# All operands of the matmuls at one remainder modulo 256 bytes, the streams of half products 192 bytes further

## The chip, the cores and the metric

The kernel runs on one NeuronCore of a Trainium2 chip. The metric is the device time of one execution in microseconds; lower is better. PE is the matrix engine, PEld its weight loads, DVE, ACT and POOL the vector, scalar and GpSimd engines, SP the queue that issues most loads.

## The reference

Three transformer-like blocks over 512 tokens of width 1024, all in float32. `first_block` runs twice, `second_block` once:

```python
for l in range(DEPTH):                                        # DEPTH = 2
    x = x + 0.5 * rms_norm(swiglu(rms_norm(x, ..), w_ffn1_in[l], w_ffn1_out[l]), ..)
    mix = token_mixing(rms_norm(x, ..), ..)                   # sliding attention, mLSTM, RWKV-7
    x = x + rms_norm(mix, ..)
    x = x + 0.5 * rms_norm(swiglu(rms_norm(x, ..), w_ffn2_in[l], w_ffn2_out[l]), ..)
    gate = jax.nn.sigmoid(rms_norm(x, ..) @ w_ple_gate[l])
    x = x + rms_norm(gate * (p[l] @ w_ple_proj[l]), ..)
...
x = x + mixed @ w_out                                         # second block: two attentions
x = x + conv_ffn(rms_norm_2(x, norm2_g), w_up, conv_w, conv_b, w_down)
```

The feed-forward width is 2816, so each `swiglu` and the `conv_ffn` has 22 tiles of 128 gate channels, 22 of 128 other channels, and an output product over 22 groups of 128.

## The kernel before, in words

Everything is held on chip between phases: `ffn` (four times), `mix` (twice), `ple` (twice), `block2` with the phase `ffn2` in it.

**Products.** A float32 factor is split into a high and a low part (`split`, L274: ACT writes the high part, DVE the rest), and `mm3` (L284) makes one product of three matmuls, high by high (L287), high by low (L288), low by high (L289). Each matmul loads its own 128 x 128 stationary operand; while one streams its moving operand, PE reads the stationary operand of the next.

**Feed-forward phases.** `norm_fast` writes the normalised tokens, transposed and split, into `xh` and `xl` [128, 8, 512]. Four tiles go the plain way (`proj_t`, the first three of them by token halves, 256 columns at a time). `fast_parts` then makes sums of quarters of the tokens, the tiles `ts`, and `fast_pair` (L451) computes the other tiles two at a time with seven products of halves: 84 matmuls of 256 columns per pair, 48 of which stream `xh` or `xl` and 36 `ts`, in the order 24 of `xh`/`xl`, 36 of `ts`, 24 of `xh`/`xl`. `ahead` (L400) splits the weights of the next pair meanwhile. The four `ffn` phases have 20 such pairs each. The phase `ffn2` has 14 (there the last 12 matmuls of a pair stream a `ts` tile too), and every third pair goes through `tile_t` (L415) instead, 12 tiles of 24 matmuls of 512 columns. `ffn_out` then multiplies by the output weights with tokens on partitions (`proj_n8`): per group of 128 channels 24 matmuls of 512 columns that stream the split weights `wh`, `wl` with the split activations `gs` as stationary operand; the last four groups keep their weights in `wx` tiles.

**Other products.** `mix` and `block2` take `xh`, `xl` from `norm_t`, as moving operand (`proj_t_steps`) or as stationary operand (`proj_n_steps`, `proj_n8`); in `mix` they are woven with the other streams, step by step.

**Order.** Each engine runs its instructions in the order in which the program has them; a matmul waits through a semaphore for the engine that wrote its operands.

**Where the tiles lie.** Pools place their tiles one behind the other in a partition, so a tile's start follows from the sizes of all before it. Remainders of the starts modulo 256 bytes in the program as built:

| tile | before | after |
|---|---|---|
| weights `wh`, `wl` | 96 | 64 |
| `xh`, `xl` from `norm_t` | 32 | 64 |
| `xh`, `xl` from `norm_fast` | 32 | 0 |
| `ts` in the four `ffn` phases / in `ffn2` | 224 / 160 | 0 |
| `gs`, and `wx` of the output products, in the four / in `ffn2` | 224 / 160 | 64 |
| `wx` of `ple` | 224 | 64 |

Steps within these tiles are multiples of 512 bytes, so every matmul on a tile has the remainder of the tile.

Of the kernel before, what the change touches and what calls it, by code (L numbers as in the profile page):

```python
# [85 lines left out]
# per-channel vectors of a layer, [128, n] columns  # L86
PV_OFF, PV_N = _offsets({k: np.zeros((1, n)) for k, n in (
    ("mu", 8), ("w0", 2), ("a0", 2), ("kk", 2), ("ka", 2), ("rk", 2), ("conv", 16))})
# per-token rows of a layer
# [7 lines left out]
def lay_out(inp):  # L97
    """The inputs in the layouts that the kernel loads: reshapes, transposes, slices and joins."""
# [4 lines left out]
    def chans(v):  # [n*128] -> [128, n]  # L103
        return v.reshape(-1, P).T
# [10 lines left out]
    def t_chunks(w):  # [K, n*128] -> [n, 128, 8, 128]  # L115
        return c(w.reshape(KD, P, -1, P).transpose(2, 1, 0, 3))

    def n_chunks(w):  # [K, n] -> [128, K/128, n]
        return c(w.reshape(-1, P, w.shape[1]).transpose(1, 0, 2))

    def halves(w):  # [K, 1024] -> [2, 128, K/128, 512]
        return c(w.reshape(-1, P, 2, 512).transpose(2, 1, 0, 3))
# [30 lines left out]
def staggered(gens, depth, lag):  # L153
    """The generators one after another, up to depth of them at a time, each lag steps behind the one before."""
    todo, live = list(gens), []
    since = lag
    while todo or live:
        if todo and len(live) < depth and (since >= lag or not live):
            live.append(todo.pop(0))
            since = 0  # L160
        for g in list(live):
            if next(g, live) is live:
                live.remove(g)
        since += 1
        yield


def weave(*streams):
    """Advance the generators together, each by its number of steps in turn (a fraction: now and then)."""
# [11 lines left out]
# products between the steps of a stream, and rates of the streams woven together  # L181
LAG, EARLY, OTHERS, DELTA, SLIDING, MLSTM = 24, 1, 2, 1, 1.3, 1
FIRST = 2  # pairs of tiles by classical products; the rest by fast_pair


class Kernel:
    def __init__(self, tc, io, out):
        self.tc, self.nc, self.io, self.out = tc, tc.nc, io, out
        self.order = list("ABCD")  # pairs of banks, those that are free first first
# [4 lines left out]
    # -------------------------------------------------------------- pools and constants  # L194
    def setup(self, es):
# [10 lines left out]
        self.ct = self.const.tile([P, C_N], F32, name="consts")  # L206

        def early_x(t):
# [5 lines left out]
                     lambda: nc.sync.dma_start(self.ct[:, P:], self.io["consts"][:, P:])]  # L214
        self.xh = self.const.tile([P, KD, S], F32R, name="xh")
        self.xl = self.const.tile([P, KD, S], F32R, name="xl")
        self.mhalf = self.const.tile([P, 16], F32, name="mhalf")
        nc.gpsimd.memset(self.mhalf, -0.5)
# [15 lines left out]
    def ring(self, **rings):  # L234
        """Name the pairs of banks that bank() takes in turn."""
        for name, tags in rings.items():
            self.rings[name] = [0, list(tags)]
# [18 lines left out]
    def small(self, n=1, tag=None):  # L256
        bufs = 4 if tag else 8
# [6 lines left out]
    # -------------------------------------------------------------- pieces  # L264
    def rsqrt(self, out, in_, scale, add, tag="rs"):
        """out = (in_ * scale + add) ** -0.5"""
# [6 lines left out]
    def split(self, h, l, src):  # L273
        """h + l = src exactly; each has 12 significant bits."""  # L274
# [9 lines left out]
    def mm3(self, out, a, b, start, stop, **kw):  # L284
        """out += a[0+1]^T b[0+1]"""
# [5 lines left out]
    def norm_begin(self):  # L291
        """Begin on the next of the norms; its tokens may come while the phase before still ends."""
        if self.norms and not self.norming:
            i, fast = self.norms.pop(0)
            self.norming = [self.gain(i), 0]
            self.raw = [self.t4.tile([P, 4, 256], F32, tag="t4", name="raw") for _ in range(2)] if fast else None
# [11 lines left out]
    def norm_token(self):  # L308
        """rms_norm(x) * gain of the next 128 tokens, transposed and split"""
# [23 lines left out]
    def norm_t(self):  # L333
        """The next norm's result, transposed and split: two tiles [128, 8, 512]"""
# [7 lines left out]
    def norm_fast(self):  # L342
        """norm_t, with what fast_parts takes"""
# [29 lines left out]
    def fast_parts(self, pool, ps, keep=False):  # L373
        """What the products of fast_pair take: B[k half][token half] = [[b11, b12], [b21, b22]] gives t1 = b12 - b11,
        t2 = b22 - t1, t3 = b22 - b12 and t4 = b21 - t2"""
# [5 lines left out]
        ts = [[pool.tile([P, 4, 256], F32R, tag=f"T{2 * i + j}", name="ts") for j in range(2)] for i in range(3)]  # L381
# [11 lines left out]
        if keep:  # L393
            t4 = [pool.tile([P, 4, 256], F32R, tag=f"T{6 + j}", name="ts") for j in range(2)]
# [6 lines left out]
    def ahead(self, jobs):  # L401
        """jobs are (what prepares, what takes that and returns what is left to do); each is prepared before the one
        before it does what is left"""
# [11 lines left out]
    def tile_t(self, xs, w, take):  # L415
        p = self.mm_ps()
        for k in range(KD):
            self.mm3(p, (w[0][:, k], w[1][:, k]), (xs[0][:, k], xs[1][:, k]), k == 0, k == KD - 1)
        return lambda: take(p)

    def fast_weights(self, w1, w2):
        """What fast_pair takes of w1 = [a11 a12] and w2 = [a21 a22], chunks [128, 8, 128]: a11, a12, s2, s1, s3, s4
        and a22, with s1 = a21 + a22, s2 = s1 - a11, s3 = a11 - a21, s4 = a12 - s2, each split"""
# [26 lines left out]
    def fast_pair(self, ws, xb, top, low):  # L450
        """[top; low] = [a11 a12; a21 a22]^T B in seven products of halves (Strassen, Winograd's form); the low half's  # L451
        first tokens stay in PSUM."""
# [31 lines left out]
    def proj_t_steps(self, xs, tiles, first=0):  # L484
        """Transposed products: tiles is a list of (chunk [128, 8, 128] in DRAM, what takes the sum).
        The first ones go by token halves, as the later tokens come later."""
# [25 lines left out]
    def proj_n_steps(self, lhs, jobs, ahead=1):  # L512
        """Products with tokens on partitions: lhs(k, t) -> (hi, lo) [128, 128]; the jobs are (w [128, 8, n] in
        DRAM, what takes (token tile, sum), its ring of banks); the pieces of w come some pairs of k ahead."""
# [25 lines left out]
    def proj_n8(self, lhs, w, kn, take, pairs, pool=None, last=4, group=3, ahead=True):  # L540
        """Products with tokens on partitions, up to 1024 columns at once: w [128, kn, n] in DRAM, pairs the
        banks of the tokens, pool(i) two tiles for the pieces of the last group, or None; take(t, sums). With
        ahead the next norm begins before the end."""
# [41 lines left out]
    def post8(self, gain, mul, room):  # L585
        """What takes y [512, 1024]: x += mul * rms_norm(y) * gain; room(t) is a tile [128, 2, 512] for y * gain"""
# [20 lines left out]
    # -------------------------------------------------------------- ffn  # L607
# [5 lines left out]
    def gs(self, pool, n):  # L613
        two = pool.tile([P, 2, S], F32R, tag=f"T{(2, 3, 0, 1, 4, 5)[n % 6]}", name="gs")
        return two[:, 0], two[:, 1]
# [14 lines left out]
    def ffn(self, l, f):  # L630
        nc, io = self.nc, self.io
        base = 8 * l + (0 if f == 1 else 4)
        with self.phase(f"ffn{l}{f}") as pool:
            pairs = self.ffn_banks()
            xs, ps = self.norm_fast()
            gpost = self.gain(base + 1)
            g = [pool.tile([P, 2, S], F32, tag=f"g{j}", name="g") for j in range(KF // 2)]
# [32 lines left out]
    # -------------------------------------------------------------- per-layer embedding  # L670
    def ple(self, l):
        nc, io = self.nc, self.io
        with self.phase(f"ple{l}") as pool:
# [6 lines left out]
            self.split(ph, pl, pt)  # L680
            pr = pool.tile([P, NT, 2, 512], F32, name="pr")
# [27 lines left out]
    # -------------------------------------------------------------- rope tables of the first block  # L709
    def rope_tables(self):  # L710
        self.load_late()
        self.cos = self.const.tile([P, NT, 8], F32, name="cos")
        self.sin = self.const.tile([P, NT, 8], F32, name="sin")
# [3 lines left out]
    def rope_tables_(self):  # L717
        """cos and sin of positions * inv_freq, [128, 4, 8]; the angles are reduced to [-pi, pi] for any
        int32 position: first by multiples of 2 pi 2^11, then of 2 pi, each constant in short parts whose
        products with the counts are exact."""  # L720
# [36 lines left out]
    # -------------------------------------------------------------- token mixing  # L757
    def mix(self, l):
# [3 lines left out]
        with self.phase(f"mix{l}") as pool:  # L762
            tl = lambda name, shape, dt=F32: pool.tile(list(shape), dt, tag=name, name=name)
            pv = tl("pv", [P, PV_N])
            nc.sync.dma_start(pv, io[f"pv{l}"])
            rows = tl("rows", [P, RW_N])
            nc.gpsimd.dma_start(rows, io[f"rw{l}"][0].partition_broadcast(P))
# [10 lines left out]
            omu = tl("omu", [P, 8])  # L778
            V.tensor_scalar(omu, pv[:, PV_OFF["mu"][0]:PV_OFF["mu"][0] + 8], -1.0, 1.0, ALU.mult, ALU.add)
            hb = tl("hb", [P, 4])  # L780
            V.tensor_scalar(hb, pv[:, PV_OFF["w0"][0]:PV_OFF["w0"][0] + 4], 0.5, None, ALU.mult)
            oka = tl("oka", [P, 2])
# [6 lines left out]
            # ---- rwkv: products, token shift  # L789
# [37 lines left out]
            def prepare():  # L827
# [7 lines left out]
                for i in range(2):  # L835
# [21 lines left out]
                    # kk, normalised by head  # L857
# [34 lines left out]
            # ---- rwkv: blocks of 128 tokens, chunks of 64  # L892
# [4 lines left out]
            def group(t):  # L897
# [9 lines left out]
                # heads of one parity share the rows of the array, and have banks of their own  # L907
# [126 lines left out]
                # group norm, bonus, gate  # L1034
# [24 lines left out]
            # ---- the other products  # L1059
# [35 lines left out]
            def others():  # L1095
# [5 lines left out]
                while len(ab) < 2:  # its tiles are prepare's before  # L1101
# [9 lines left out]
            # ---- the three together  # L1111
# [6 lines left out]
            # ---- out  # L1118
# [18 lines left out]
    def sliding(self, pool, qk, va, sinks, out):  # L1137
# [3 lines left out]
        for t in range(NT):  # L1141
            # rope
# [11 lines left out]
            # split, scaled by 1/8 for q, and transposed  # L1154
# [88 lines left out]
    def mlstm(self, pool, X, conv, vo, iff, row, out):  # L1243
# [3 lines left out]
        # gates, tokens on partitions  # L1247
# [7 lines left out]
        # log sigmoid(f) = -log(1 + e), e = exp(-f); log(1 + e) = e * log(w) / (w - 1), w = fl(1 + e)  # L1255
# [8 lines left out]
        # heads on partitions: G = cumsum(log f), a = i - G, M = cummax(a)  # L1264
# [396 lines left out]
```

## Time and profile before

| | us |
|---|---|
| median of three runs | 2948.43 |
| lowest, highest | 2946.67, 2959.89 |
| span of the profiled execution, first to last instruction | 2960.7 |
| PE busy in it | 2898.4 |
| DVE, ACT, POOL busy | 1953.1, 1425.6, 140.3 |

The profile is of one execution; no time other than its span is recorded for it. The page's slices show PE at nine tenths or more from the second on and DMA engines busy between none and four tenths. A busy PE is not PE at its peak: matmuls are pipelined, so the busy times of two that follow each other overlap. Their starts don't.

### The profile page before, as it was taken

How to read it: one execution, taken by the hardware profiler on the slowest of the kernel's cores; microseconds unless marked ns; L12 is line 12 of the kernel's file. 1: busy time of each engine (PE TensorE's matmuls, PEld its weight loads, DVE VectorE, ACT ScalarE, POOL GpSimd, SP SyncE). 2: the span in 40 equal slices, each digit the busy share in tenths (PEclk: the TensorE clock that was granted, in tenths of full speed). 3: DMA queues.
4: the chain of work that ended last, by engine and by line, in shares of the span. 5: the costliest groups of instructions: out<-in, count | busy, mean ns of one | idle time of the engine just before them, and what ended most of it. 6: DMA issues, size and time to landing. Idle time of an engine off the chain costs nothing. (4 is left out here: it accounts for less than half of the span.)

```text
span 2960.7 us, 47335 instructions
## 1 busy us (share of the span) xinstructions
PE 2898.4 (98%) x19000; PEld 2538.6 (86%) x19000; DVE 1953.1 (66%) x3464; ACT 1425.6 (48%) x2784; POOL 140.3 (5%) x169
## 2 busy tenths in 40 slices
PE   7999999999999999999999999999999999999999
PEld 7998887877999878999887877799987877789987
DVE  7884555756888357886345655688635766688853
ACT  5663343343666245555334233456534456566641
POOL 0000000101000000000000000100000220000000
PEclk9999999999999999999999988999999999999999
DMA  4333322002233332333412000233343210313332
GB/s 152 108 122 103 97 81 65 8 8 65 93 115 115 100 103 90 109 107 116 130 56 79 15 8 29 75 107 111 114 128 90 93 43 1 93 62 104 100 101 91
DMA packets 74156, 250.91 MB, mean 85 GB/s; under 512 B 8112, under 2 KB 10416, under 8 KB 73680
## 3 DMA queue, kind: packets, MB, share of 16 engines
q1 hardware_dynamic: 70992, 236.99, 25.2%
q0 software_dynamic: 2944, 10.90, 1.1%
q8 instruction: 149, 2.44, 0.3%
q14 instruction: 71, 0.58, 0.1%
HBM read 245.76 MB, written 2.10 MB: 84 GB/s over the span
## 5 line engine op out<-in xcount | busy, mean ns | idle before, releaser
L276 DVE TENSOR_TENSOR wl<-raw,wh 128x1024 fp32r<-128x1024 f32 (+2 forms) x218 | 259.2, 1193 | 410.1 <-ACT wh L275 408.5
L275 ACT CAST wh<-raw 128x1024 fp32r<-128x1024 f32 (+2 forms) x218 | 223.4, 1026 | 469.9 <-PE psone L289 316.9
L287 PE MATMUL psfast<-xh,wh 128*128 128x256 f32 x1448 | 401.9, 278 | 0.0
L289 PE MATMUL psfast<-xh,wl 128*128 128x256 f32 x1448 | 400.7, 277 | 0.0
L288 PE MATMUL psfast<-xl,wh 128*128 128x256 f32 x1448 | 400.6, 277 | 0.0
L287 PE MATMUL psfast<-ts,wh 128*128 128x256 f32 x1184 | 333.1, 282 | 0.0
L289 PE MATMUL psfast<-ts,wl 128*128 128x256 f32 x1184 | 333.0, 281 | 0.0
L288 PE MATMUL psfast<-ts,wh 128*128 128x256 f32 x1184 | 332.5, 281 | 0.0
L288 PE MATMUL psone<-wl,gs 128*128 128x512 f32 x720 | 284.2, 395 | 0.0
L289 PE MATMUL psone<-wh,gs 128*128 128x512 f32 x720 | 284.1, 395 | 0.0
L287 PE MATMUL psone<-wh,gs 128*128 128x512 f32 x720 | 282.3, 395 | 0.0
L287 PEld LDWEIGHTS psfast<-xh,wh 128*128 128x128 f32 x1448 | 272.0, 188 | 1.3
L288 PEld LDWEIGHTS psfast<-xl,wh 128*128 128x128 f32 x1448 | 272.1, 188 | 0.5
L289 PEld LDWEIGHTS psfast<-xh,wl 128*128 128x128 f32 x1448 | 272.0, 188 | 0.0
L435 ACT CAST wh<-raw 128x512 fp32r<-128x512 f32 x282 | 174.7, 621 | 157.8 <-PE psfast L288 154.2
L287 PEld LDWEIGHTS psfast<-ts,wh 128*128 128x128 f32 x1184 | 222.7, 188 | 0.7 <-ACT top L465 0.7
L289 PEld LDWEIGHTS psfast<-ts,wl 128*128 128x128 f32 x1184 | 222.9, 188 | 0.0
L288 PEld LDWEIGHTS psfast<-ts,wh 128*128 128x128 f32 x1184 | 222.8, 188 | 0.0
L437 DVE TENSOR_TENSOR wl<-raw,wh 128x1024 fp32r<-128x1024 f32 (+1 forms) x188 | 179.1, 953 | 64.9 <-ACT wh L435 64.5
L287 PE MATMUL psmm<-xh,wh 128*128 128x256 f32 (+1 forms) x616 | 206.8, 338 | 0.1
L288 PE MATMUL psmm<-xl,wh 128*128 128x256 f32 (+1 forms) x616 | 205.8, 335 | 0.0
L289 PE MATMUL psmm<-xh,wl 128*128 128x256 f32 (+1 forms) x616 | 204.3, 333 | 0.0
(545 smaller groups left out, 6494.1 us busy)
## 6 DMA issues: line engine op xcount, KB each, us to landing
raw<-f1i SPq DMA_DIRECT2D x88, 512.0 KB, 3.5
raw<-f2i SPq DMA_DIRECT2D x88, 512.0 KB, 3.5
raw<-f1o SPq DMA_DIRECT2D x44, 512.0 KB, 3.7
raw<-f2o SPq DMA_DIRECT2D x44, 512.0 KB, 3.9
raw<-w2u SPq DMA_DIRECT2D x44, 512.0 KB, 3.5
raw<-w2d SPq DMA_DIRECT2D x22, 512.0 KB, 3.9
gain<-gains POOLq DMA_DIRECT2D x19, 512.0 KB, 4.0
raw<-wr SPq DMA_DIRECT2D x16, 512.0 KB, 3.6
```

Of the source, the lines that this page charges most:

```text
L275: self.rounded = self.nc.scalar.copy(h, src)
L276: self.nc.vector.tensor_sub(l, src, h.bitcast(F32))
L287: mm(out, a[0], b[0], start=start, stop=False, **kw)
L288: mm(out, a[0], b[1], start=False, stop=False, **kw)
L289: mm(out, a[1], b[0], start=False, stop=stop, **kw)
L435: nc.scalar.copy(h[:, i], src[:, i])
L437: sub(l, src, h.bitcast(F32))
```

## The change

It computes the same products. Starts of tiles move, by changed tile sizes and by tiles that only fill:

- `consts`, `pv`, `rows`, `hg` and `cv` get longer rows than they use, three small vectors of `mix` become one tile `vecs`, `cos` and `sin` move into `setup`, and tiles called `pad` are added, so that the tiles behind them begin at the remainder 64.
- `xh` and `xl` get 48 more floats (192 bytes), and there are two `places` in them: from 0 for the plain norms, from 48 for the norms of the feed-forward phases. `norm_begin` picks one.
- The tiles of `ts` have 1088 floats instead of 1024 and begin with their float 48; `gs` takes the same tiles from their start.
- `tile_t` makes its product by two halves of 256 columns.
- `small` keeps four buffers instead of eight for untagged tiles of more than one column.
- Comments are gone, which shifts line numbers.

```diff
         self.x = self.const.tile([P, NT, D], F32, name="x")
-        self.ct = self.const.tile([P, C_N], F32, name="consts")
+        self.ct = self.const.tile([P, 2416], F32, name="consts")
...
-        self.xh = self.const.tile([P, KD, S], F32R, name="xh")
-        self.xl = self.const.tile([P, KD, S], F32R, name="xl")
+        xh = self.const.tile([P, KD * S + 48], F32R, name="xh")
         self.mhalf = self.const.tile([P, 16], F32, name="mhalf")
+        xl = self.const.tile([P, KD * S + 48], F32R, name="xl")
+        self.cos = self.const.tile([P, NT, 8], F32, name="cos")
+        self.sin = self.const.tile([P, NT, 8], F32, name="sin")
+        self.const.tile([P, 16], F32, name="pad")
+        self.places = [[z[:, o:o + KD * S].rearrange("p (k n) -> p k n", k=KD) for z in (xh, xl)] for o in (0, 48)]
...
     def small(self, n=1, tag=None):
-        bufs = 4 if tag else 8
+        bufs = 4 if tag or n > 1 else 8
...
             self.norming = [self.gain(i), 0]
+            self.xh, self.xl = self.places[fast]
...
-        ts = [[pool.tile([P, 4, 256], F32R, tag=f"T{2 * i + j}", name="ts") for j in range(2)] for i in range(3)]
+        room = lambda i: pool.tile([P, 1088], F32R, tag=f"T{i}", name="ts")[:, 48:1072].rearrange(
+            "p (k n) -> p k n", k=4)
+        ts = [[room(2 * i + j) for j in range(2)] for i in range(3)]
...
         p = self.mm_ps()
-        for k in range(KD):
-            self.mm3(p, (w[0][:, k], w[1][:, k]), (xs[0][:, k], xs[1][:, k]), k == 0, k == KD - 1)
+        for cs in slice(0, 256), slice(256, 512):
+            for k in range(KD):
+                self.mm3(p[:, cs], (w[0][:, k], w[1][:, k]), (xs[0][:, k, cs], xs[1][:, k, cs]), k == 0, k == KD - 1)
...
-        two = pool.tile([P, 2, S], F32R, tag=f"T{(2, 3, 0, 1, 4, 5)[n % 6]}", name="gs")
-        return two[:, 0], two[:, 1]
+        two = pool.tile([P, 1088], F32R, tag=f"T{(2, 3, 0, 1, 4, 5)[n % 6]}", name="gs")
+        return two[:, 0:S], two[:, S:2 * S]
...
-            cv = pool.tile([P, 4, 44], F32, name="cv")
-            nc.sync.dma_start(cv, io["cv2"].rearrange("p (j m) -> p j m", j=4))
+            cv = pool.tile([P, 4, 56], F32, name="cv")
+            nc.sync.dma_start(cv[:, :, 0:44], io["cv2"].rearrange("p (j m) -> p j m", j=4))
```

The order on the engines is the same but for two places in the phase `ffn2`. On PE, where the first of its `tile_t` tiles begins (`psmm` is its sum in PSUM), before:

```order
L288 MATMUL psfast<-ts,wh 128x256
L289 MATMUL psfast<-ts,wl 128x256
L287 MATMUL psmm<-xh,wh 128x512
L288 MATMUL psmm<-xl,wh 128x512
L289 MATMUL psmm<-xh,wl 128x512
```

and now:

```order
L293 MATMUL psfast<-ts,wh 128x256
L294 MATMUL psfast<-ts,wl 128x256
L292 MATMUL psmm<-xh,wh 128x256
L293 MATMUL psmm<-xl,wh 128x256
L294 MATMUL psmm<-xh,wl 128x256
```

Where 24 matmuls of 512 columns stood per tile, 48 of 256 stand now, 24 for each half of the tokens. On DVE, at the same tiles (`z` are sums of the next pair's weights, `g` the result of the tile), before:

```order
L444 TENSOR_TENSOR z<-raw 128x512
L1587 SCALAR_TENSOR_TENSOR g<-psmm,cv,g 128x511
L437 TENSOR_TENSOR wl<-s,wh 128x1024
L1588 SCALAR_TENSOR_TENSOR g<-psmm,cv,g 128x511
L445 TENSOR_TENSOR z<-raw,s 128x512
```

and now:

```order
L453 TENSOR_TENSOR z<-raw 128x512
L454 TENSOR_TENSOR z<-raw,s 128x512
L1595 SCALAR_TENSOR_TENSOR g<-psmm,cv,g 128x511
L446 TENSOR_TENSOR wl<-s,wh 128x1024
L1596 SCALAR_TENSOR_TENSOR g<-psmm,cv,g 128x511
```

The second subtraction into `z` moved ahead of the work on the tile, by three instructions, six times in the phase.

## Rows read from the trace of the kernel before

**Rows 1.** The page: span, and busy time (share of the span) by engine.

```profile
span 2960.7 us, 47335 instructions
...
PE 2898.4 (98%) x19000; PEld 2538.6 (86%) x19000; DVE 1953.1 (66%) x3464; ACT 1425.6 (48%) x2784; POOL 140.3 (5%) x169
```

**Rows 2.** PE's waits, longest total first: releaser, total us, times, longest.

```profile
PE pstr L321 <- DVE xn L316: 22.1, 15, 10.8
...
```

**Rows 3.** Work per stretch: length, busy us and count per engine, granted clock, DMA share, GB/s.

```profile
240.33:340.76 100.43, 100.43 (x435) 81.34 (x434) 38.65 (x43) 31.26 (x40) 0.00 (x0) 1.00 0.40 121
1475.68:1491.78 16.10, 16.10 (x73) 13.33 (x71) 8.71 (x14) 6.06 (x14) 1.65 (x3) 1.00 0.16 56
1126.78:1143.34 16.56, 16.56 (x72) 13.35 (x71) 11.13 (x17) 9.67 (x18) 1.11 (x2) 1.00 0.30 96
62.26:71.99 9.73, 9.73 (x86) 9.73 (x85) 8.26 (x13) 5.86 (x13) 0.00 (x0) 1.00 0.31 102
```

**Rows 4.** The costliest group of PE over the span: form, count, busy us, mean ns.

```profile
L287 PE MATMUL psfast<-xh,wh 128*128 128x256 f32 x1448 | 401.9, 278 | 0.0
...
```

**Rows 5.** Order of time on PE: start, duration, instruction; ends of the stretches of 512 columns.

```profile
240.33 0.39 PE L287 MATMUL psone<-wh,gs 128*128 128x512 f32 x1
...
340.76 0.40 PE L287 MATMUL psone<-wx,gs 128*128 128x512 f32 x1
...
1110.06 0.39 PE L289 MATMUL psone<-wh,xl 128*128 128x512 f32 x1
...
1126.55 0.39 PE L289 MATMUL psone<-wh,xl 128*128 128x512 f32 x1
1126.78 0.39 PE L287 MATMUL psone<-wx,xh 128*128 128x512 f32 x1
...
1143.34 0.40 PE L289 MATMUL psone<-wx,xl 128*128 128x512 f32 x1
...
1475.68 0.39 PE L287 MATMUL psone<-wx,gs 128*128 128x512 f32 x1
...
1491.78 0.39 PE L289 MATMUL psone<-wx,gs 128*128 128x512 f32 x1
```

**Rows 6.** The same view, first `ffn`: ends of a stretch of `xh`, and of 17 pairs.

```profile
62.28 0.28 PE L287 MATMUL psfast<-xh,wh 128*128 128x256 f32 x1
...
67.73 0.28 PE L287 MATMUL psfast<-ts,wh 128*128 128x256 f32 x1
...
227.64 0.28 PE L287 MATMUL psfast<-xh,wh 128*128 128x256 f32 x1
```

**Rows 7.** The same view, start of the first `ffn`'s first pair.

```profile
45.40 0.28 PE L287 MATMUL psfast<-xh,wh 128*128 128x256 f32 x1
...
48.23 0.29 PE L287 MATMUL psfast<-ts,wh 128*128 128x256 f32 x1
...
52.55 0.28 PE L287 MATMUL psfast<-xh,wh 128*128 128x256 f32 x1
```

**Rows 8.** The same view, `ffn2`: two `tile_t` tiles, an early pair, a late pair.

```profile
2646.68 0.39 PE L287 MATMUL psmm<-xh,wh 128*128 128x512 f32 x1
...
2657.87 0.28 PE L287 MATMUL psfast<-xh,wh 128*128 128x256 f32 x1
...
2667.62 0.28 PE L287 MATMUL psfast<-xh,wh 128*128 128x256 f32 x1
...
2782.38 0.28 PE L287 MATMUL psfast<-xh,wh 128*128 128x256 f32 x1
...
2792.28 0.28 PE L287 MATMUL psfast<-xh,wh 128*128 128x256 f32 x1
```

**Rows 9.** The same view, `ffn2`: the first products behind a stall.

```profile
2737.03 0.39 PE L287 MATMUL psfast<-xh,wh 128*128 128x256 f32 x1
2737.26 0.28 PE L288 MATMUL psfast<-xl,wh 128*128 128x256 f32 x1
2737.37 0.28 PE L289 MATMUL psfast<-xh,wl 128*128 128x256 f32 x1
```

More of the change, by code (lines that the diff above doesn't have):

```diff
@@ L213, in setup @@
         self.late = [lambda: early_x(2), lambda: early_x(3),
-                     lambda: nc.sync.dma_start(self.ct[:, P:], self.io["consts"][:, P:])]
-        self.xh = self.const.tile([P, KD, S], F32R, name="xh")
-        self.xl = self.const.tile([P, KD, S], F32R, name="xl")
+                     lambda: nc.sync.dma_start(self.ct[:, P:C_N], self.io["consts"][:, P:])]
+        xh = self.const.tile([P, KD * S + 48], F32R, name="xh")
         self.mhalf = self.const.tile([P, 16], F32, name="mhalf")
+        xl = self.const.tile([P, KD * S + 48], F32R, name="xl")
[3 more added lines that the diff above has]
+        self.places = [[z[:, o:o + KD * S].rearrange("p (k n) -> p k n", k=KD) for z in (xh, xl)] for o in (0, 48)]
         nc.gpsimd.memset(self.mhalf, -0.5)
@@ L393, in fast_parts @@
         if keep:
-            t4 = [pool.tile([P, 4, 256], F32R, tag=f"T{6 + j}", name="ts") for j in range(2)]
+            t4 = [room(6 + j) for j in range(2)]
         def late():
@@ L636, in ffn @@
             gpost = self.gain(base + 1)
+            pool.tile([P, 32], F32, name="pad")
             g = [pool.tile([P, 2, S], F32, tag=f"g{j}", name="g") for j in range(KF // 2)]
@@ L680, in ple @@
             self.split(ph, pl, pt)
+            pool.tile([P, 32], F32, name="pad")
             pr = pool.tile([P, NT, 2, 512], F32, name="pr")
@@ L711, in rope_tables @@
         self.load_late()
-        self.cos = self.const.tile([P, NT, 8], F32, name="cos")
-        self.sin = self.const.tile([P, NT, 8], F32, name="sin")
         with self.phase("rope"):
@@ L763, in mix @@
             tl = lambda name, shape, dt=F32: pool.tile(list(shape), dt, tag=name, name=name)
[L764 to L767, printed above, removed]
+            pv = tl("pv", [P, 40])
+            nc.sync.dma_start(pv[:, 0:PV_N], io[f"pv{l}"])
+            rows = tl("rows", [P, 800])
+            nc.gpsimd.dma_start(rows[:, 0:RW_N], io[f"rw{l}"][0].partition_broadcast(P))
             lora = tl("lora", [P, 512])
@@ L777, in row @@
                 return rows[:, o:o + n]
-            omu = tl("omu", [P, 8])
+            vecs = tl("vecs", [P, 24])
+            omu, hb, oka = vecs[:, 0:8], vecs[:, 8:12], vecs[:, 16:18]
             V.tensor_scalar(omu, pv[:, PV_OFF["mu"][0]:PV_OFF["mu"][0] + 8], -1.0, 1.0, ALU.mult, ALU.add)
-            hb = tl("hb", [P, 4])
             V.tensor_scalar(hb, pv[:, PV_OFF["w0"][0]:PV_OFF["w0"][0] + 4], 0.5, None, ALU.mult)
-            oka = tl("oka", [P, 2])
             V.tensor_scalar(oka, pv[:, PV_OFF["ka"][0]:PV_OFF["ka"][0] + 2], -1.0, 1.0, ALU.mult, ALU.add)
@@ L1345, in block2 @@
             cc = lambda n: c2[:, C2_OFF[n][0]:C2_OFF[n][0] + C2_OFF[n][1]]
-            hg = tl("hg", [P, 256])
-            nc.gpsimd.dma_start(hg, io["hg2"][0].partition_broadcast(P))
+            hg = tl("hg", [P, 288])
+            nc.gpsimd.dma_start(hg[:, 0:256], io["hg2"][0].partition_broadcast(P))
             b0, b1, b2, b3 = self.order
```

## The prediction

> **What bounds the kernel now.** I read the busy table first: PE is busy 2898.4 us of a span of 2960.7, DVE 1953.1 [rows 1]. PE's waits by releaser come next: the largest, the transposes of the norms waiting for DVE, is 22.1 us in all, and the other 22 entries of that view are smaller [rows 2]. So PE's own pace sets the end nearly everywhere. The work per stretch shows how much cover the other engines leave: in one pair of tiles of the fast products (9.73 us) DVE is busy 8.26 and ACT 5.86; in the first eighteen groups of an output product (100.43 us) DVE is busy 38.65 and the DMA share is 0.40 [rows 3]. The granted clock is 1.00 in both, so nothing here is a clock matter.
>
> The busy time of a matmul in the grouped view (278 ns for `psfast<-xh` [rows 4]) is not its price, since matmuls overlap. The price is the step from one start to the next, which I take from the first and the last row of a stretch and the number of matmuls between them, known from the code. What separates stretches of one shape is where the operands lie. Call D the moving operand's start minus the next stationary operand's start, modulo 256 bytes (both remainders are in the table of the kernel before).
>
> - 512 columns, D = 128: 340.76 - 240.33 over 432 steps is 232.5 ns. D = 192: 1143.34 - 1126.78 over 71 is 233.2. D = 64: 1126.55 - 1110.06 over 72 is 229.0. D = 0: 1491.78 - 1475.68 over 71 is 226.8 [rows 5].
> - 256 columns, D = 192: 67.73 - 62.28 over 48 is 113.5. The ts products (D = 128) behind them bring a whole pair of 84 to (227.64 - 62.28) / 17 pairs = 9.727 us [rows 6], so 36 of them take 9.727 - 5.45 = 4.28 us, 118.8 each.
>
> The two stretches of 71 are the same loop and the same weight tiles `wx`, with 8.71 and 11.13 us of DVE inside [rows 3]; the addresses differ, and 6.4 ns of a step with them. Worst D for 512 columns (192) is best for 256. The change puts 512-column products at D = 0 and products of halves at D = 192.
>
> **A second pace at D = 192.** The first 24 products of the first layer run at (48.23 - 45.40) / 24 = 117.9 ns, also with D = 192 [rows 7]. In the last feed-forward phase a whole pair takes 2667.62 - 2657.87 = 9.75 us early on and 2792.28 - 2782.38 = 9.90 later, 117.9 a step, although neither program nor addresses changed [rows 8]. Between the two lies a start after a stall, where the first step is 0.23 us and the next is 0.11 [rows 9]. So products of halves have two settled paces at the same addresses, 113.5 and 117.9, and the slow one survives from there to the end of that phase. In the four ffn phases it is the ts products at D = 128 that never let a pace stand: each time behind them the stream comes back to 113.5. The change removes exactly these. What a phase falls into at its start it will then keep for its 20 pairs.
>
> **The change part by part.** All of this is PE time with no wait in it, so it shortens the path one for one.
>
> (a) Fast products of the four ffn phases, 80 pairs at 9.727 us now. At the fast pace 84 x 113.5 = 9.534: -15.5 us. At the slow pace 9.904: +14.1. One phase of 20 pairs: -3.9 or +3.5, a swing of 7.4.
>
> (b) The last phase has 14 such pairs, about half at 9.75 and half at 9.90, 137.5 us. Fast: 14 x 9.534 = 133.5, -4.0. Slow: 138.7, +1.1.
>
> (c) `tile_t` cuts its 12 tiles into halves: 288 matmuls at (2657.87 - 2646.68) / 48 = 233.1 ns [rows 8] become 576. Fast: 65.4 against 67.1 us, -1.8; slow 67.9, +0.8. The 288 more weight loads need no term, since in the stretch of pairs PEld is loaded for every 256 columns already and the 113.5 holds with it.
>
> (d) Output products: 432 matmuls per feed-forward phase. Four phases: 100.43 to 432 x 226.8 = 97.98, -2.45 each, -9.8. The fifth has D = 192 now, 233.2: 432 x 6.4 = -2.8. Together -12.6. The last 96 of each phase are at D = 0 already.
>
> (e) Products that take xh from the plain norm: 236 with `wx` at D = 192 now, 236 x 6.4 ns = -1.5; 432 transposed ones in the mix phases from 233.2 to between 226.8 and 231, as they are cut short by other work, -1.7; some 1200 at D = 64, 2.2 ns each, of which I count half for the same reason, -1.3.
>
> (f) One loss: 288 products of halves in the mix phases go from D = 192 to D = 0, which has no long stretch here. The bounds are 113.5 and the worst stretch of 256 columns, (52.55 - 48.23) / 36 = 120.0 [rows 7]: 0 to +1.9, taken +1.0.
>
> (g) Costs at nothing: the norms' writes to the other place of `xh` follow transposes that PE runs behind the last readers anyway; DVE's moved `z` subtraction falls into a pair in which DVE is idle 1.47 us (9.73 - 8.26 [rows 3]), 1.27 at 9.534; the smaller ring of `small` holds the four tiles that one prepare uses; the `cv` load in 176-byte pieces is needed only behind the first tile of products, 24 steps after they begin. If such a cover failed, it would be one wait each, of the size of those counted in [rows 2]. A bare wait of PE on PE behind each pair of tiles in the last phase: six times, between 0 and the 0.11 us by which a first step after a stall is longer, under 0.7 us.
>
> 512 columns and (f): -12.6 - 1.5 - 1.7 - 1.3 + 1.0 = **-16.1**. Halves, all fast: -15.5 - 4.0 - 1.8 = -21.3. The first ffn started slow in the trace with the same addresses and the same order that it keeps, while the pairs behind the start of the last phase are at the fast pace [rows 8]; so I take one phase of five slow: -21.3 + 7.4 = **-13.9**. Sum -30.0 us.
>
> **Against the pages.** The stretches above have a step that depends on where the two operands of PE lie [rows 5]. The Trainium skill's page "SBUF — State Buffer", section "Who interferes with whom", says that PE has two independent read ports and never waits on anyone, and its page "TensorE: Matmul & The Clock Gate", section "Step-by-step: what each phase is for", that loading the next weights takes no read bandwidth from the running matmul. By that rule the change would give nothing, which is the second rival below; the trace does not agree, by 6.4 ns per step between the two `wx` stretches.
>
> **The rivals.** *The slow pace wins.* With three to five of the five phases in the slow pace the halves cost -21.3 + 22.2 = +0.9 to +15.7, and the whole gain is 15.2 to 0.4 us: 2933 to 2948. For it: nothing but a stall resets the pace once the ts products lie at D = 192, and half of the last phase shows it. Against it: the last phase was fast from its start to the stall, for half of its pairs.
>
> *The address is not the cause.* ts, gs and wx are different tiles, and their paces could follow the tile (when it was written, say) rather than its remainder. Then nothing moves but (c): 2947 to 2949. Against it: `wx`, written and used by the same lines in both stretches, runs at 226.8 and at 233.2.
>
> *Slower.* A stream at one D may settle at neither pace but at the worst one of the trace, 120.0 ns [rows 7]: 8472 products of halves (7896 in pairs, 576 tiles' halves) at 120.0 are 1016.6 us against 778.2 + 137.5 + 67.1 = 982.8 now, +33.8 - 16.1 = +17.7: 2966. It decides from (982.8 + 16.1) / 8472 = 117.9 ns on, which is the slow pace itself: any pace above it loses. It is seen only behind D = 128, in one stretch.
>
> **How the numbers follow.** The median of the runs shown is 2948.4, 12.3 below the span of the profiled execution; I take the same difference off both: span 2960.7 to 2930.7, median **2918.4**. Chances: the forecast, with no to two phases slow (2911 to 2926), 0.78; slow pace in three or more 0.13; address no cause 0.05; slower 0.04. The range from 2905 (all fast, all of (e), and a little for the 113.5, whose 48 steps hold the recovery behind ts) to 2938 leaves out some 0.15. Faster by over 0.5% (14.7 us, about what can be told from no change) means below 2933.7: the forecast and a part of three phases slow, 0.82; same 0.14; slower 0.04.
>
> **What would show it.** Right: 432 output products in 98.0 us; the last `wx` stretches unchanged at 226.8; pairs of 84 in either 9.53 or 9.90 us and nothing between, constant through a phase; DVE, ACT and DMA busy times as before. Wrong: output products still over 230 ns (D is no cause), a pace for halves over 118, or pairs that switch between the two paces without a stall.

## The result, and the profile after

| | before | after |
|---|---|---|
| median (times of the runs), us | 2954.16 (2946.67, 2948.43, 2959.89, 2962.16) | 2911.48 (2910.41, 2910.74, 2912.22, 2919.21) |
| span of the profiled execution | 2960.7 | 2917.4 |
| ratio of the times, 95% interval | | 0.9873, 0.9843 to 0.9903 |

Faster by 1.3%. The profiled execution of after is the slowest of its four, and that of before, by its span, is one like its slower two; both have their reason in the rows below. A phase is called slow below when its pairs of 84 run at 9.89 us, fast when they run at 9.52.

The page of after, to be set beside [rows 1]: PE's busy time falls by 45 us, that of DVE and ACT stays, and 288 matmuls have come in.

```profile
span 2917.4 us, 47905 instructions
...
PE 2853.4 (98%) x19288; PEld 2525.3 (87%) x19288; DVE 1952.8 (67%) x3464; ACT 1425.8 (49%) x2784; POOL 141.6 (5%) x169
```

The work per stretch of after (columns as in [rows 3]: length, then busy us and count of PE, PEld, DVE, ACT, POOL, then the granted clock, DMA share, GB/s). First the 432 products of the first output product, the `wx` stretch of the first `ple`, 17 pairs of the first `ffn` and 17 pairs of the third:

```profile
235.38:333.59 98.21, 98.21 (x434) 80.90 (x433) 38.86 (x43) 31.48 (x40) 0.00 (x0) 1.00 0.41 123
...
1113.40:1129.73 16.33, 16.33 (x73) 13.47 (x72) 11.03 (x17) 9.84 (x18) 1.11 (x2) 1.00 0.33 98
...
44.77:206.62 161.85, 161.85 (x1430) 161.84 (x1428) 139.31 (x220) 99.34 (x204) 0.00 (x0) 1.00 0.34 109
1167.23:1335.42 168.19, 168.19 (x1430) 168.19 (x1429) 140.07 (x220) 99.48 (x204) 0.00 (x0) 1.00 0.33 105
```

The first line was 100.43 us in [rows 3], with the same DVE and ACT work inside: 227.3 ns a step instead of 232.5. The second is the stretch that was at D = 192: 72 steps of 226.8 ns now. The last two lines are the same 17 pairs of the same code at the same addresses: 161.85 / 17 = 9.52 us a pair in the first phase (also in the second and fourth), 168.19 / 17 = 9.89 in the third. DVE, ACT and the clock are the same in both. The second pace is there, and one of the four phases has fallen into it.

**The clock.** The two `mix` phases run one program. From the end of the output product before to the first pair of the phase behind it, in before and in after:

```profile
357.13:769.79 412.66, 400.03 (x2638) 331.28 (x2636) 255.95 (x610) 167.92 (x373) 35.28 (x40) 0.98 0.15 46
1492.01:1923.89 431.88, 419.37 (x2638) 346.89 (x2637) 252.40 (x587) 167.42 (x371) 35.03 (x40) 0.93 0.14 44
```

```profile
349.92:762.85 412.93, 400.65 (x2637) 333.69 (x2636) 256.10 (x610) 167.80 (x373) 35.24 (x40) 0.98 0.15 46
1479.68:1893.20 413.52, 400.87 (x2637) 333.83 (x2636) 252.53 (x587) 167.50 (x371) 35.31 (x40) 0.98 0.15 46
```

The second one of before is 19.2 us longer than its twin, at a mean clock of 0.93. The reason is one stretch in which PE is granted 0.50, its 1.2 GHz level; after has it too, shorter. PE was busy without a gap at the full clock ahead of it in both (10.90 of 10.90 us, 10.85 of 10.85). Before, then after:

```profile
1743.00:1753.90 10.90, 10.90 (x84) 9.09 (x85) 4.60 (x16) 6.02 (x21) 1.27 (x1) 1.00 0.01 2
...
1753.90:1805.10 51.20, 51.20 (x239) 39.99 (x238) 17.30 (x63) 12.61 (x40) 1.13 (x1) 0.50 0.00 1
```

```profile
1750.00:1760.85 10.85, 10.85 (x86) 9.11 (x86) 5.43 (x27) 2.06 (x10) 0.00 (x0) 1.00 0.01 2
1760.85:1774.50 13.65, 13.65 (x57) 11.25 (x57) 6.12 (x19) 4.91 (x17) 1.14 (x1) 0.50 0.01 2
```

So of the 43.3 us between the two spans an estimated 18 are clock and not the change: the second `mix` differs by 18.4 us between the two, the first by 0.3. In two later runs below, shift32 and d16, only 3.4 us at 0.50 stand there, and their second `mix` takes 408.5 and 408.1 us. The executions whose times are too low to hold that long stretch compare as 2946.67 and 2948.43 with 2910.41 to 2912.22: 36.4 us between the means of these. That is the worth of the change where no phase is slow. With slow phases in some executions it is less: against the later runs of before the medians of after differ by 32.8 us (2945.78, 2912.97) and 33.1 (2945.30, 2912.23).

### The profile page after: what moved, and what is told of

It reads as the page before. It is cut to its first block, busy times and chain, and to the rows that moved or that the text cites. A ratio compares the mean times of both kernels' runs of the same rounds, so it can differ in the third digit from the quotient of the medians.

```text
span 2917.4 us, 47905 instructions
## 1 busy us (share of the span) xinstructions
PE 2853.4 (98%) x19288; PEld 2525.3 (87%) x19288; DVE 1952.8 (67%) x3464; ACT 1425.8 (49%) x2784; POOL 141.6 (5%) x169
## 3 DMA queue, kind: packets, MB, share of 16 engines
q0 software_dynamic: 2944, 10.90, 1.1%
## 5 line engine op out<-in xcount | busy, mean ns | idle before, releaser
L292 PE MATMUL psfast<-ts,wh 128*128 128x256 f32 x1184 | 328.7, 278 | 0.5
L293 PE MATMUL psfast<-ts,wh 128*128 128x256 f32 x1184 | 328.0, 277 | 0.0
L294 PE MATMUL psone<-wh,gs 128*128 128x512 f32 x720 | 280.2, 389 | 0.0
L292 PE MATMUL psone<-wh,gs 128*128 128x512 f32 x720 | 278.4, 389 | 0.0
L292 PE MATMUL psmm<-xh,wh 128*128 128x256 f32 (+1 forms) x712 | 222.1, 314 | 0.6 <-ACT xh L280 0.4
L293 PE MATMUL psmm<-xl,wh 128*128 128x256 f32 (+1 forms) x712 | 220.9, 311 | 0.0
L294 PE MATMUL psmm<-xh,wl 128*128 128x256 f32 (+1 forms) x712 | 219.6, 309 | 0.0
```

Source lines behind the costliest of these rows:

```text
L292: mm(out, a[0], b[0], start=start, stop=False, **kw)
L293: mm(out, a[0], b[1], start=False, stop=False, **kw)
L294: mm(out, a[1], b[0], start=False, stop=stop, **kw)
```

## The experiments

The theory of the prediction: D, the moving operand's start minus the next stationary operand's, modulo 256 bytes, sets the step; 256 columns at D = 192 have two paces; products of another D between them keep bringing the fast one back. Rivals: the tile counts and not its address; the remainder itself counts and not the difference; the slow phase has another cause.

### map: steps by D alone

One moving tile `M`, one set of stationary tiles `W`, stretches behind a stall each (the first product of each has `K`, which ACT writes from the sum of the stretch before):

```python
for i in range(count):
    sr, mr = srs[i % len(srs)] // 4, mrs[i % len(mrs)] // 4
    w = K[:, sr:sr + 128] if s == 0 and i == 0 else W[:, sr + 128 * (i % 8):sr + 128 * (i % 8) + 128]
    b = mr + 512 * (i % 6)
    mm(p[:, 0:n], w, M[:, b:b + n], start=i == 0, stop=i == count - 1)
```

> This kernel computes none of the reference: it streams one moving tile against one set of stationary tiles, in stretches of 48 to 72 matmuls of one shape with one difference D (moving start minus next stationary start, modulo 256 bytes), each stretch behind a short stall, D in steps of 16 bytes; then stretches of D = 192 with other D ahead and no stall, the same D at other remainders, and two remainders in turn. If D sets the step: 512 columns 226.8 ns at D = 0, 229 at 64, 232.5 at 128, 233.2 at 192, the same when both starts move by 64 or 96 bytes or the moving one by 256; 256 columns at D = 192 either 113.5 or 117.9, one of them for a whole stretch, and at 128 near 119 to 120; a stretch with stationary starts in turn at D = 0 and 192 alternates 226.8 and 233.2. If the remainder itself counts and not the difference, the moved stretches have other steps. If the tile counts and not its address, all stretches of one shape have one step.

The order of time on PE has one row for a stretch: start, duration, count. The last product of a row lasts 0.39 us (512 columns) or 0.28 (256), the rest is steps. 512 columns at D = 64, 192, then 0 and 128 with both starts moved by 96 bytes:

```profile
62.35 10.93 PE L68 MATMUL a512d<-M,W 128*128 128x512 f32 x47
...
157.52 11.12 PE L68 MATMUL a512d<-M,W 128*128 128x512 f32 x47
...
922.15 10.84 PE L68 MATMUL r_512d<-M,W 128*128 128x512 f32 x47
...
940.30 11.07 PE L68 MATMUL r_512d<-M,W 128*128 128x512 f32 x47
```

(11.12 - 0.39) / 46 is 233.3 ns, (10.84 - 0.39) / 46 is 227.2 with the first steps in it. 256 columns at D = 0, 112, 128 and 192:

```profile
205.24 7.24 PE L68 MATMUL a256d<-M,W 128*128 128x256 f32 x59
...
260.03 6.88 PE L68 MATMUL a256d<-M,W 128*128 128x256 f32 x59
...
267.61 7.17 PE L68 MATMUL a256d<-M,W 128*128 128x256 f32 x59
...
299.13 7.11 PE L68 MATMUL a256d<-M,W 128*128 128x256 f32 x59
```

The settled steps (from the ninth on) of all D, ns, in this kernel (D = 0 of 512 columns from the moved stretches):

| D | 0 | 16 | 32 | 48 | 64 | 80 | 96 | 112 | 128 | 144 | 160 | 176 | 192 | 208 | 224 | 240 |
|---|---|---|---|---|---|---|---|---|---|---|---|---|---|---|---|---|
| 512 columns | 226.7 | 231.7 | 233.3 | 233.4 | 228.9 | 231.1 | 233.3 | 231.1 | 232.2 | 233.3 | 234.3 | 233.3 | 233.3 | 234.7 | 233.3 | 233.3 |
| 256 columns | 120.0 | 113.3 | 116.7 | 118.3 | 117.8 | 119.9 | 120.0 | 113.3 | 118.7 | 118.7 | 118.7 | 119.2 | 113.3, 117.8 | 119.3 | 118.3 | 117.2 |

D is the cause: one tile pair, addresses alone changed, and the steps of the kernel come back, 226.7, 228.9, 232.2 and 233.3. With both starts moved by 64 or 96 bytes, or the moving one by 256, they are the same to 1.3 ns. D = 0, the best for 512 columns, is the worst of this table for 256. D = 192 gave 113.3 in 35 stretches and 117.8 in 7, each one pace to its end. One product at D = 0 or 128 between two stretches at D = 192, and 36 at D = 0, 64, 128 or 240, left the pace at 113.3. One at D = 64 was enough to turn it, without any stall, both times that it was tried (48 at D = 192, one at 64, 72 at 192: 113.7, then 117.7 ns):

```profile
800.55 5.51 PE L68 MATMUL ma_256d<-M,W 128*128 128x256 f32 x47
805.90 0.28 PE L68 MATMUL mb_256d<-M,W 128*128 128x256 f32 x1
806.02 8.64 PE L68 MATMUL mc_256d<-M,W 128*128 128x256 f32 x72
```

One expectation fell. With stationary starts in turn the steps were 226, 226, 236, 232 and again, not 226.8 and 233.2 in turn, though their mean, 230.0, is as expected. With moving starts in turn at D = 0 and 192 the steps were 225 to 229, on average 226.7. So D gives the step of a stream in which D is constant; what mixed streams do, it doesn't say, and no run here settles that. Nor does any run show why the difference matters inside PE.

### ts128, gs128, shift32: one part undone, one thing moved

```diff
ts128
-        room = lambda i: pool.tile([P, 1088], F32R, tag=f"T{i}", name="ts")[:, 48:1072].rearrange(
+        room = lambda i: pool.tile([P, 1088], F32R, tag=f"T{i}", name="ts")[:, 32:1056].rearrange(
gs128
-        return two[:, 0:S], two[:, S:2 * S]
+        o = 32 if n < 18 else 0
+        return two[:, o:o + S], two[:, o + S:o + 2 * S]
shift32
-        self.ct = self.const.tile([P, 2416], F32, name="consts")
+        self.ct = self.const.tile([P, 2408], F32, name="consts")
```

> The changed kernel with the ts tiles 64 bytes earlier, so that their products stand at D = 128 as in the kernel before; all else as changed. If D sets the step, a pair of 84 takes 9.73 us again in every phase, with 24 products of xh at 113.5 ns behind each group of ts products and no phase at 9.89; 94 pairs by 9.727 - 9.534 are 18.1 us more than the 2910.4 us of the changed kernel with all phases fast, 2928 us. If the slow phase has another cause than the missing return, one of the phases may still stand at 9.89. If the address is no cause: 2910 to 2919, as the changed kernel.

> The changed kernel with the gs tiles of the first 18 groups of every output product 128 bytes further, so that their 432 matmuls per phase stand at D = 128. If D sets the step: 232.5 ns against 226.8, 5 x 432 x 5.7 = 12.3 us more, 100.4 us per stretch of 432 instead of 98.0 and 2923 us with all halves fast (each slow phase 7 more). If the address is no cause: no difference, 2910 to 2919 us.

> The changed kernel with every tile behind the constants 32 bytes earlier: all remainders differ, no difference D does. If only D counts: 2910 to 2919 us as the changed kernel, the steps the same to 0.3 ns. If the remainder itself counts (128 x 512 of the moving operand from 32 instead of 64), steps of the 512-column products differ from 227 by up to some ns: 2160 x 2 ns would be 4 us and more. The number of phases at 9.89 us a pair may differ between executions in either case.

Measured beside 14 runs of before with a median of 2946.29: ts128 2929.53 to 2933.64, median 2931.76; gs128 2924.16 to 2940.02, median 2927.60; shift32 2905.13 to 2941.85, median 2913.13. The stretches that answer, in this order: 17 pairs of ts128 (third phase), the first 432 output products of gs128, those of shift32 and its first 17 pairs.

```profile
1177.20:1342.56 165.36, 165.36 (x1429) 165.35 (x1428) 139.61 (x220) 99.38 (x204) 0.00 (x0) 1.00 0.30 107
```

```profile
234.02:334.49 100.47, 100.47 (x435) 81.17 (x434) 38.81 (x43) 31.49 (x40) 0.00 (x0) 1.00 0.39 123
```

```profile
234.96:333.18 98.22, 98.22 (x434) 80.88 (x433) 38.85 (x43) 31.52 (x40) 0.00 (x0) 1.00 0.41 123
44.35:206.19 161.84, 161.84 (x1429) 161.84 (x1428) 139.35 (x220) 99.45 (x204) 0.00 (x0) 1.00 0.33 109
```

ts128: 165.36 / 17 = 9.73 us, the pace of [rows 6], and that in all four phases: neither 9.52 nor 9.89 occurs in them, but for 9.87 in the last pair of each, which has a stall in it. gs128: 100.47 us, back to [rows 3]. shift32: other remainders everywhere and the steps of after to 0.01 us per stretch; its three executions above 2920 us have mean clocks of 0.979 to 0.985, the other seven 0.992 and more. The rivals of the tile and of the remainder itself fall; two parts of the change are undone one by one, each at its price.

### entry, d16, d0, after_again: which D for the halves

Since D = 16 had given 113.3 three times out of three and settled within two steps, I took it for a D with one pace, and for a better place for the halves than 192. `entry` is the streaming kernel with 20 entries behind stalls of different length; d16 and d0 move the places of the changed kernel:

```diff
d16
-        ... for o in (0, 48)]
+        ... for o in (0, 4)]
-        room = lambda i: pool.tile([P, 1088], F32R, tag=f"T{i}", name="ts")[:, 48:1072].rearrange(
+        room = lambda i: pool.tile([P, 1088], F32R, tag=f"T{i}", name="ts")[:, 4:1028].rearrange(
d0
-        ... for o in (0, 48)]
+        ... for o in (0, 0)]
-        room = lambda i: pool.tile([P, 1088], F32R, tag=f"T{i}", name="ts")[:, 48:1072].rearrange(
+        room = lambda i: pool.tile([P, 1088], F32R, tag=f"T{i}", name="ts")[:, 0:1024].rearrange(
```

> Computes none of the reference: the streaming kernel again, 256 columns mostly. D = 192, 16 and 112 are each entered 20 times behind stalls of different length; D = 16 and 112 also without a stall behind products at D = 128, 64 and 192; D in steps of 4 bytes around 16; and three stretches of 400 products. If the moment of entry chooses the pace at D = 192, its 20 stretches divide between 113.3 and 117.8 ns and each keeps its pace to the end, the one of 400 too; if D = 16 and D = 112 have one settled pace only, all of theirs are at 113.3, whatever stands ahead. Rival: every D has two paces and the first kernel's three entries at D = 16 fell on the fast one by chance; then some of the 20 are at 117 or more.

> The changed kernel with the streams of half products 16 bytes from the stationary start instead of 192: xh and xl of the feed-forward phases from float 4, ts from float 4. If the step follows D and D = 16 has one pace only: every pair of 84 at 9.52 us in all five phases, no phase at 9.89, so 2905 to 2911 us in nearly every execution, 3 to 4 us below the changed kernel's mean where that has one slow phase in two executions. If two paces exist here too: as the changed kernel, some phases at 9.89. If the offset of 192 bytes was needed for another reason than the pace: slower than the changed kernel.

> The changed kernel without the 192 bytes: one remainder for everything, the half products at D = 0 too. If D sets the step: pairs of 84 at 84 x 120.0 = 10.08 us, (10.08 - 9.53) x 94 = 51.7 us more in the pairs and 576 x 6.7 = 3.8 in the tiles by halves, near 2966 us, slower than the kernel before. If one common remainder is what helps and the 192 bytes are not needed: 2910 to 2920.

> The changed kernel as it is, on the same chip as the others of this call. Every execution has five feed-forward phases that each fall into one of two paces: 2905 to 2911 us where all are fast, 7.3 us more for each slow one, so 2905 to 2942 with most between 2905 and 2920. If the slow phase of the first profile was a single accident: all within 2905 to 2912.

Rows of `entry` in the order 192, 16, 112, 16, 192, 112 (time order on PE, stretches of 47):

```profile
32.98 5.50 PE L58 MATMUL e256d<-M,W 128*128 128x256 f32 x47
...
39.26 5.65 PE L58 MATMUL e256d<-M,W 128*128 128x256 f32 x47
...
45.69 5.54 PE L58 MATMUL e256d<-M,W 128*128 128x256 f32 x47
...
58.30 5.80 PE L58 MATMUL e256d<-M,W 128*128 128x256 f32 x47
...
71.22 5.70 PE L58 MATMUL e256d<-M,W 128*128 128x256 f32 x47
...
84.16 5.52 PE L58 MATMUL e256d<-M,W 128*128 128x256 f32 x47
```

D = 192: 15 of the 20 stretches at 113.3 ns, 5 at 117.8 (5.70). Ahead of all but the first of them stands the same D = 112; what the program changes from one to the next is the length of the stall and the PSUM buffer. D = 16: none at 113.3, but 116.7 (5.65), 118.7 and 120.0 (5.80). D = 112: all 20 at 113.3 once settled (5.54 holds some slower first steps), and also without a stall behind D = 128, 64 and 192. My reading of D = 16 was wrong, and with it the forecast of 2905 to 2911 us for d16: the three entries of the first kernel were alike, and so was what came of them. The long stretches keep their pace to the end: 399 products at D = 192 in (45.40 - 0.28) / 398 = 113.4 ns each, at D = 16 in 120.0.

```profile
680.21 45.40 PE L58 MATMUL g256d<-M,W 128*128 128x256 f32 x399
...
726.46 48.04 PE L58 MATMUL g256d<-M,W 128*128 128x256 f32 x399
```

The kernels, beside runs of before with a median of 2945.78: d16 2921.90 to 2939.52, median 2931.14; d0 2964.41 to 2984.50, median 2968.02, ratio 1.0081 (1.0049 to 1.0113); after_again 2906.74 to 2921.57, median 2912.97. 17 pairs of d16's first and third phase, then of d0's first:

```profile
44.89:206.74 161.85, 161.85 (x1430) 161.85 (x1429) 139.33 (x220) 99.30 (x204) 0.00 (x0) 1.00 0.33 109
1167.61:1334.22 166.61, 166.61 (x1430) 166.60 (x1428) 139.47 (x220) 99.38 (x204) 0.00 (x0) 1.00 0.34 106
```

```profile
44.92:216.28 171.36, 171.36 (x1430) 171.35 (x1429) 140.88 (x220) 99.28 (x204) 0.00 (x0) 1.00 0.33 103
```

d16 falls into 9.52 or 166.61 / 17 = 9.80 us a pair, 116.7 ns a step as in `entry`; in two of its four `ffn` phases it is the latter. d0 stands at 10.08 us, 120.0 ns, everywhere, 22 us slower than before: one remainder for all operands, without the 192 bytes, loses. The time was forecast at 2966.

### d112, after_third: one pace

The same two lines with 28 floats (112 bytes) instead of 48.

> The changed kernel with the streams of half products 112 bytes from the stationary start instead of 192. In the streaming kernels 27 of 27 stretches at D = 112 settled at 113.3 ns, whatever stood ahead, against 56 of 68 at D = 192. If that holds in the kernel: every pair of 84 at 9.52 us in all five phases in every execution, so 2905 to 2912 us, no execution near 2916 or 2921 but for the clock, 2 to 5 us below the changed kernel's mean. Rival: the streams of the kernel, with stalls inside and several tiles, have settled paces that the streaming kernels do not show, as at D = 16; then whole phases stand above 9.52 us a pair, and the time is 2915 or more.

> The changed kernel as it is, beside the run at D = 112. Each slow phase is worth 7.4 us: executions near 2907 to 2910 (none), 2914 to 2917 (one), 2921 to 2924 (two), more only where the granted clock is lower; about half of them near the lowest, as in the six before (2906.7, 2909.1, 2909.6, 2916.3, 2917.5, 2921.6).

Beside runs of before with a median of 2945.30: d112 2903.26, 2905.12, 2906.84, 2908.51; after_third 2905.40, 2909.97, 2910.35, 2914.12, 2919.97, 2927.10. Ratios to before: 0.9870 (0.9856 to 0.9884) and 0.9898 (0.9879 to 0.9917). 17 pairs of d112's third phase; then of after_third's first and second, whose profile is of its slowest execution:

```profile
1164.97:1326.81 161.84, 161.84 (x1429) 161.83 (x1428) 139.44 (x220) 99.33 (x204) 0.00 (x0) 1.00 0.34 109
```

```profile
44.28:212.47 168.19, 168.19 (x1430) 168.19 (x1429) 139.90 (x220) 99.40 (x204) 0.00 (x0) 1.00 0.33 105
771.28:933.12 161.84, 161.84 (x1429) 161.84 (x1428) 140.11 (x221) 99.34 (x204) 0.00 (x0) 1.00 0.33 112
```

All phases in the profiled execution of d112 are fast, and five of the six executions of after lie above the slowest of d112. It beats the median of after by 6 us beside it; the two intervals still overlap a little. What the changed kernel's own profiles show fits: one slow `ffn` phase in the first (2919.21), none in after_again's (2909.13), two in after_third's (2927.10). Of its 16 executions nine lie at 2905.4 to 2912.2 and seven from 2914.1 to 2927.1. At that rate four low ones in a row would come about one time in ten, so that d112 never has a slow phase rests more on the 27 entries of the streaming kernels than on its four times.

## Why the prediction was right, and where not

**What bounds it, and the second rival.** Right. PE's pace sets the end; in the four `ffn` phases shorter steps came out one for one. But "no wait in it" did not hold for every pair of the last phase (see (b)). That the address is no cause is refuted by `map` and by gs128: the step changes by 6.6 ns of 233.3 by the start address alone. The Trainium skill's pages "SBUF — State Buffer" ("Who interferes with whom") and "TensorE: Matmul & The Clock Gate" ("Step-by-step: what each phase is for") say that PE's two read ports are independent and that the weight load takes no read bandwidth from the running matmul; a step that follows the difference of the two operands' starts does not agree with that.

**(a) Pairs.** Both paces are where the rows put them: 9.52 and 9.89 us for 9.534 and 9.904. The fast one was a little high, since the 48 steps of [rows 6] hold the recovery behind `ts`: settled it is 113.33. "Nothing between, constant through a phase" held for 19 pairs of 20. The last of each phase has a stall, and in the slow phase that stall turned the pace. Its rows there, at the 60th product (118 ns steps, one of 0.22 us behind the stall), are followed by 23 steps to 1365.16 of 114.3 ns on average:

```profile
1362.03 0.28 PE L293 MATMUL psfast<-ts,wh 128*128 128x256 f32 x1
1362.15 0.28 PE L294 MATMUL psfast<-ts,wl 128*128 128x256 f32 x1
1362.31 0.38 PE L292 MATMUL psfast<-xh,wh 128*128 128x256 f32 x1
1362.53 0.28 PE L293 MATMUL psfast<-xl,wh 128*128 128x256 f32 x1
```

A stall there doesn't always turn the pace to fast: in the two slow phases of after_third the same one left it at 117.8, and in the second phase of gs128 it turned a fast stream slow.

That the `ts` products at D = 128 were what kept the old phases uniform is shown by ts128, in the kernel itself. Its last phase starts slow, with 24 products in 2.83 us (117.9 ns each); behind 36 of `ts` the next 12 take 1.38 us (115.0 ns with the recovery, 113 to 114 at their end):

```profile
2598.21 0.28 PE L292 MATMUL psfast<-xh,wh 128*128 128x256 f32 x1
...
2601.04 0.29 PE L292 MATMUL psfast<-ts,wh 128*128 128x256 f32 x1
...
2605.36 0.28 PE L292 MATMUL psfast<-xh,wh 128*128 128x256 f32 x1
...
2606.74 0.28 PE L292 MATMUL psfast<-ts,wh 128*128 128x256 f32 x1
```

**(b), (c) The last phase.** It changes pace at its stalls, as forecast from [rows 8, 9]. Two tiles by halves take 10.88 us in five of six places and 11.31 in one, for 11.19 before [rows 8]: -0.3 or +0.1 each, -1.5 in all for -1.8. The 14 pairs gave less than forecast, 139.5 us (forecast without their waits as 137.5) to 137.9: -1.6, and -2.3 in after_again, where all of them are fast, for -4.0. Every second pair has a wait at its 25th product, for ACT's `top` by the profile, and the wait took up what the steps gave: the two steps there take 0.46 us before (2670.35 to 2670.81) and 0.59 after (2632.26 to 2632.85). Such a pair before, after, and then two tiles by halves after:

```profile
2667.62:2677.76 10.14, 10.14 (x87) 9.90 (x85) 9.24 (x14) 7.31 (x15) 0.00 (x0) 1.00 0.38 114
```

```profile
2629.54:2639.65 10.11, 10.02 (x87) 9.69 (x85) 9.27 (x14) 7.38 (x15) 0.00 (x0) 1.00 0.37 110
...
2609.14:2620.02 10.88, 10.88 (x98) 10.88 (x97) 10.42 (x14) 5.32 (x10) 0.00 (x0) 1.00 0.41 130
2731.26:2742.57 11.31, 11.31 (x98) 11.31 (x97) 10.36 (x14) 5.57 (x10) 0.00 (x0) 1.00 0.37 135
```

**(d) Output products.** 98.2 us for 97.98, and the fifth the same, where 100.8 stood: -2.2 four times and -2.6, together -11.5 for -12.6. The 226.8 of [rows 5] is from `wx` tiles; the stretch of 432 stays half a nanosecond above it, and no run here looked for the reason.

**(e) Plain norm.** The `wx` stretches of the two `ple` phases took 16.33 us each, 0.46 less than 72 steps of 233.2 ns. Of those at D = 64, 288 in a row in `block2` took 65.31 us, 65.93 before: 226.8 and 228.9 a step. The others of this term were not separated.

**(f) The loss.** A mis-sized term of the sum, small like (d): the price is at its upper bound. In the first `mix`, 102 halves in a row with the same work beside them, before and after:

```profile
374.03:385.99 11.96, 11.92 (x105) 11.73 (x104) 7.94 (x25) 5.17 (x9) 0.00 (x0) 1.00 0.15 50
```

```profile
366.81:379.40 12.59, 12.57 (x106) 12.37 (x104) 8.12 (x25) 5.17 (x9) 0.00 (x0) 1.00 0.13 48
```

0.63 / 102 = 6.2 ns each, and behind the first stall the steps are 120 ns throughout for 113 to 114 before; 1.8 us for all 288, taken 1.0. The 120.0 of [rows 7] was of another D, 128, and of one short stretch; `map` shows that D = 0 settles at just that. Before a price is halved between its bounds, the bound should have to be shown unlikely, and nothing did.

**The slow phases.** The forecast allowed one of five; the median execution, by its time, has none or next to none (its trace is not kept). That is the 7 us between 2918.4 and 2911.5: the all-fast sum was -37.4, and the comparison without the long half-clock stretch gives -36.4. That these two lie so close is in part luck, since misses cancel: in after_again the four `ffn` phases, from their first pair to the output product, take 190.62 us each for 194.93 and three times 194.77 before, -16.8 for the -15.5 of (a), while (b) to (d) gave less than forecast. The rival of three and more slow phases was right in its mechanism: each costs 168.19 - 161.85 = 6.3 us per 17 pairs, 7.3 and 7.4 per phase in after and after_third, for a swing of 7.4; none of the profiled executions has more than two slow ones among its four `ffn` phases. The "slower" rival named a settled pace of 120.0, which exists, but at D = 0 and not at 192; d0 is what it describes, at 2968.

**The clock, a step that failed.** "Nothing here is a clock matter" was read from two stretches of 9.73 and 100.43 us. The page of before shows two slices at 8 in its clock line, and the view of cores a mean of 0.986. The 12.3 us between its span and the median, carried over as if they were a constant, are less than the 19.2 us by which the `mix` with those 51.2 us at 0.50 is longer than its twin. The forecast didn't suffer: the same 12.3 us stood on both sides, so that it is the median less 30.0.

## What to carry to other kernels

Read the step from start to start for every stretch of back-to-back matmuls, and group by the difference of the two operands' starts; where equal shapes have unequal steps, a few bytes of padding are worth some 3 to 6% of the step. The best difference depends on the width: here 0 for 512 columns, 112 for 256, and the best for one is bad for the other. Before a difference is taken over, enter it many times behind different stalls: three equal readings at D = 16 were one state, not a law.

## What the runs showed of the hardware that was not expected

- Streams of 256 columns with constant addresses settle into one of several exact paces, which differ from entry to entry and then hold for hundreds of products (in `entry` they differ in the stall ahead and the PSUM buffer; what chooses the pace no run isolates): 113.33 or 117.8 ns at D = 192; 113.3, 116.7, 118.7 or 120.0 at D = 16; always 113.33 at D = 112 (27 entries behind stalls or other products in the two streaming kernels).
- Steps of 4 bytes matter: 256 columns at D = 8 took 126.7 ns and at D = 104 130.0, the worst seen, while their neighbours 0, 16, 96 and 112 gave 113.3 to 120.0.
- Starts that alternate do not follow the rule of constant D: moving starts in turn at D = 0 and 192 ran at 226.7 on average, not at the mean of 226.7 and 233.3.
- The granted clock fell to 0.50 for 51.2 us in before and 13.65 in after, in the second `mix`, out of stretches in which PE was busy without a gap at 1.00.
